# The second layer's normalised rows transposed once, and their sums formed from the transposed quarters

## The chip, the cores and the metric

The kernel runs on one core of one Trainium2 chip. The metric is the time of one execution in microseconds (us) on the device, as the median of several runs; smaller is better. The engines are called by their names in the profile: PE is TensorE's matmul, PEld its weight load, DVE is VectorE, ACT is ScalarE, POOL is GpSimd, SP is SyncE, which here only starts DMAs.

## What is computed

Two layers of an encoder over 512 tokens of width 1024, in float32. Each layer normalises its input, projects it into heads and a gate, runs a token mixer (layer 0: dilated sliding windows; layer 1: grouped-query attention with rotary over a grid), attends to 256 memory tokens, gates the heads and adds an output projection to the residual stream:

```python
for i in range(DEPTH):
    h = rmsnorm(x, norm_g[i])
    mem_h = rmsnorm(mem, mem_norm_g[i])
    proj = einsum('bsd,de->bse', h, w_in[i])           # heads, memory queries, gate
    o_mix = mixer_dilated(...) if i % 2 == 0 else mixer_axial_gqa(...)
    o_mem = memory_attention(q_mem, mem_h, w_mem_kv[i], ...)
    y = concatenate([o_mix, o_mem], axis=-1) * silu(gate)
    x = x + einsum('bse,ed->bsd', y, w_out[i])
```

The change sits between the two layers: where the x that layer 0 has just produced is normalised and brought into the form in which layer 1's projections read it.

## The kernel before

**Split matmuls.** TensorE multiplies in a shortened float32 (fp32r). Every operand is therefore kept as a high part (a rounded copy) and a low part (the value minus the high part), and each product is three matmuls (`mm3`, L162 to L165: high x high, high x low, low x high). `split` (L155) makes the two parts: ScalarE copies the high part, VectorE subtracts it to get the low one.

**Weights.** `Weights` streams weight tiles of 128 x 1024. For each, SP starts the load (`dma`, L233), ScalarE makes the high part `wh` (`hi`, L285), and VectorE the low part `wo` (`lo`, L295). ScalarE can only make the next high part once TensorE is done with the tile four earlier (RING). `advance` (L311) is called after each group of matmuls and issues up to two low parts, one weight sum, up to two high parts and new loads. A group of matmuls with the advance and the tick behind it is called a slot here.

**S chunks.** A large projection is not one matrix product but seven products of quarter matrices (`s_chunk`, L352, in the order of PRODUCTS, L350), as in Strassen's scheme: the activations are cut into four quarters, 11 and 12 (first half of the tokens, first and second half of the columns), 21 and 22 (second half of the tokens), and the seven left operands are 12, 11, S1 = 21 - 22, S2 = S1 - 11, S4 = 12 + S2, S3 = 11 - 21, and 22. The weights have such sums too (T1 to T4); in the later chunks they are formed by DMAs that add onto a tile, started on GpSimd's queue (`sum`, L238: T1 at L247, T2 at L257, T3 at L264, T4 at L269). An activation operand is held with its columns on the partitions, so it has to be transposed, high and low part in one 128 x 2048 tile.

**The order of the work** is written out by the kernel's own driver (`Driver`, L41). Every group of matmuls ends with a `tick`. A generator that was handed over with `spawn` is stepped in a tick, behind the weights' `advance` of that slot; one handed over with `release` has its first step in `free`, which runs right behind the matmuls and in front of `advance`; its later steps run in ticks. What a generator yields is the number of slots until its next step. `late` puts an instruction at the end of the tick, `soon` at the start of the next. Each engine works strictly in the order in which its instructions were written.

**Around the change.** `out_proj` (L810) of layer 0 ends in `out_rest` (L694): `chunk` (L331) runs 2 x 4 groups, one per half n of the columns and block b of 128 tokens, and spawns `ev` per group with a delay of 2, which adds the product to the residual `acc` (L705). For n = 1 it goes on into `ev_o` (L1189): store the block to `x1d` (L1192), sum of squares (ScalarE) and reciprocal root (GpSimd) in `norm_1` (L450), the scaling in `norm_2` (L463, two instructions of VectorE), and then the operands for layer 1. For b < 2 `put_h` (L495) transposes and splits 12 and 11. For b >= 2 `sum_h` (L504) forms S1 in natural layout, `sums_h` (L509) puts S1 and forms S2, S3 and S4 in natural layout, and after the last block `rest_h` (L519) puts S2, S4, S3 and 22, one per slot. Each `put_h` of a block of 128 tokens is four 128 x 128 transposes into a PSUM bank (`turn4`, L467), one ScalarE copy and one VectorE subtraction of 128 x 512. The pauses between the steps are the numbers in EO (L30).

Behind `out_proj` come the memory tokens' projections (`mem_kv`, L593), two times four groups of twelve matmuls: keys (`ev_k`: squares on ScalarE, reciprocal root on GpSimd, scaling on VectorE, transpose, split) and values (`ev_v`: high part, and one slot later the low part, both read from the PSUM bank). `setup_b` (L1221) builds the rotary table of layer 1 in four steps, the first SET_B ticks after its spawn. Then the first S chunk of layer 1 (memory queries, `ev_qmb`) begins with the operand 12.

Of the kernel before, what the change touches and what calls it, by code (L numbers as in the profile page):

```python
# [10 lines left out]
F32 = mybir.dt.float32  # L11
F32R = mybir.dt.float32r
AF = mybir.ActivationFunctionType
ALU = mybir.AluOpType
# [8 lines left out]
NBIG, NM4, NS2, SCRATCH = 7, 23, 13, 2048  # L23
RING, LEAD = 4, 2
XW, BOTH = (1, 2, 0, 5), False
BULK, ACTIVE, MEM_AT, SET_AT, WARM, MEM_B, PREP_Y, ACC_AT, PREP_B, HALF, SET_B = 2, 2, 5, 15, 1, 12, 1, 4, 1, {"a": 3, "b": 3, "o": 0}, 3
MEM_STEP = 1, 1
MEM_D = 4
PD, W_EARLY = 1, True
EO = 1, 2, 2, 2, 1  # L30
YB = {"m": (2, 2), "k": (1, 1, 1), 0: (1, 2, 1), 1: (1, 2, 1)}
Y = [3, 2, 2, 2, 3, 2, 2, 1, 1, 1]

# [91 lines left out]
def trunk_kernel(ctx: ExitStack, tc: tile.TileContext, x, mem, wall, norm_g, mem_norm_g, gcol,  # L125
                 qn_a, kn_a, qn_b, kn_b, ident_d, mask_d, tab_a, tab_b, out):
    nc = tc.nc
    V, A, G, T = nc.vector, nc.scalar, nc.gpsimd, nc.tensor
# [6 lines left out]
    drv = Driver()  # L135

    def big(dt=F32, name="big"):
        return pool.tile([128, 2048], dt, tag="big", name=name, bufs=NBIG)

    def m4(dt=F32, name="m4"):  # L140
        return pool.tile([128, 1024], dt, tag="m4", name=name, bufs=NM4)

    def s2(dt=F32, name="s2"):
        return pool.tile([128, 512], dt, tag="s2", name=name, bufs=NS2)

    def pj(name="pj"):
        return psum.tile([128, 512], F32, tag="pj", name=name, bufs=4)

    def at(name="at"):
        return psum.tile([128, 512], F32, tag="at", name=name, bufs=4)  # L150
# [4 lines left out]
    def split(hi, lo, src, act=True):  # L155
        if act:
            A.copy(hi, src)  # L157
        else:
            V.tensor_copy(hi, src)
        V.tensor_tensor(lo, src, hi.bitcast(F32), ALU.subtract)  # L160
# [170 lines left out]
    def chunk(units, nb, group, evac):  # L331

        ps = [None] * nb
        for u in range(units):
            w = []
            for h, l in (W.take(), W.take()):
                w += [(h[:, k * 512:(k + 1) * 512], l[:, k * 512:(k + 1) * 512]) for k in range(2)]
            for b in range(nb):
                if u == 0:
                    ps[b] = pj()  # L340
                group(w, u, b, ps[b])
                drv.free()
                W.advance()
                if u == units - 1:
                    drv.spawn(evac(b, ps[b]), 2)
                drv.tick()

    n_half = [0]
# [101 lines left out]
    def norm_1(xb, both=False):  # L450

        ss = sm(2, "ss")
        for j in range(2):
            jk = s2(name="sq")
            if both and j:
                V.tensor_tensor_reduce(jk, xb[j], xb[j], 1.0 / 1024.0, 0.0, ALU.mult, ALU.add, ss[:, j:j + 1])
            else:
                A.activation(jk, xb[j], AF.Square, scale=1.0 / 32.0, accum_out=ss[:, j:j + 1])
        r, e = sm(1, "rstd"), sm(1, "mse")
        G.tensor_tensor(e, ss[:, 0:1], ss[:, 1:2], ALU.add)  # L460
        return rstd_of(e, 1)

    def norm_2(xb, r, row, js=(0, 1)):  # L463
        for j in js:
            V.scalar_tensor_tensor(xb[j], xb[j], r, row[j], ALU.mult, ALU.mult)

    def turn4(src, hi, lo, mid=None):  # L467

        p = at("xT")
        for k in range(4):  # L470
            T.transpose(p[:, k * 128:(k + 1) * 128], src[:, k * 128:(k + 1) * 128], ident)  # L471
        if mid:
            mid()
        split(hi, lo, p.rearrange("p (k t) -> p k t", k=4))

    def norm_3(xb, dst, c0, j):
        cs = slice(c0, c0 + 128)
        turn4(xb[j], dst.block(0, j, cs), dst.block(1, j, cs))
# [6 lines left out]
    def proj_t(act, sels, evac):  # L485

        def group(w, u, b, p):
            for k in range(4):
                kk = 4 * u + k
                mm3(p, sels[b](act, 0, kk), sels[b](act, 1, kk), w[k][0], w[k][1], kk == 0, kk == 7)  # L490
        chunk(2, len(sels), group, evac)

    part = {}

    def put_h(H, k, c, src, mid=None, early=False):  # L495

        if c == 0:
            part[k] = big(F32R, "h" + k).rearrange("p (a k t) -> p a k t", a=2, k=4)
        if c or early:
            H[k] = part[k]  # L500
        cs = slice(c * 128, (c + 1) * 128)
        turn4(src, part[k][:, 0, :, cs], part[k][:, 1, :, cs], mid)

    def sum_h(low):  # L504
        s1 = s2(name="xs1")
        V.tensor_tensor(s1, low[0], low[1], ALU.subtract)
        return s1

    def sums_h(H, top, low, c, s1, sums):  # L509

        (a11, a12), a21 = top, low[0]
        s2_, s4 = s2(name="xs2"), s2(name="xs4")
        put_h(H, "S1", c, s1)
        V.tensor_tensor(s2_, s1, a11, ALU.subtract)
        V.tensor_tensor(a21, a11, a21, ALU.subtract)
        V.tensor_tensor(s4, a12, s2_, ALU.add)
        sums.append((s2_, s4, a21, low[1]))

    def rest_h(H, sums, d=1):  # L519
        for i, k in enumerate(("S2", "S4", "S3", "22")):  # L520
            for c in range(2):
                put_h(H, k, c, sums[c][i])
            yield d

    def head_sq(p, n=4):
        ss = sm(n, "hss")
        for j in range(n):
            jk = small.tile([128, 128], F32, tag="junk", name="junk", bufs=2)
            A.activation(jk, p[:, j * 128:(j + 1) * 128], AF.Square, scale=QS, accum_out=ss[:, j:j + 1])  # L529
        return rstd_of(ss, n)  # L530

    def head_mul(p, r, n=4, dst=None):
        xn = (s2(name="xn") if dst is None else dst).rearrange("p (a b) -> p a b", a=4)
        V.tensor_tensor(xn[:, 0:n], p.rearrange("p (a b) -> p a b", a=4)[:, 0:n],  # L534
                        r[:, 0:n, None].to_broadcast([128, n, 128]), ALU.mult)
        return xn

    def transpose4(xn, n=4):
        p = at("qT")
        for j in range(n):  # L540
            T.transpose(p[:, j * 128:(j + 1) * 128], xn[:, j, :], ident)
        return p.rearrange("p (a b) -> p a b", a=4)
# [44 lines left out]
    def put_norm(q, gain, hi, lo):  # L587

        drv.late(lambda: A.activation(hi, q, AF.Copy, scale=gain))
        drv.soon(lambda: V.scalar_tensor_tensor(lo, q, gain, hi.bitcast(F32), ALU.mult, ALU.subtract))  # L590
        yield 1

    def mem_kv(layer, M):  # L593
        kt_ = [m4(F32R, "kmT").rearrange("p (h t) -> p h t", h=4) for _ in range(2)]
        vt_ = [m4(F32R, "vm").rearrange("p (b e) -> p b e", b=2) for _ in range(2)]

        def ev_k(b, p):
            r = head_sq(p)
            yield 2
            xn = head_mul(p, r)  # L600
            yield 2
            q = transpose4(xn)
            cs = slice(b * 128, (b + 1) * 128)
            yield from put_norm(q, gk_m[layer], kt_[0][:, :, cs], kt_[1][:, :, cs])

        def ev_v(b, p):

            A.activation(vt_[0][:, b], p, AF.Copy, scale=0.5)
            yield 1
            V.scalar_tensor_tensor(vt_[1][:, b], p, 0.5, vt_[0][:, b].bitcast(F32), ALU.mult, ALU.subtract)  # L610

        proj_t(M, NAT[:2], ev_k)
        proj_t(M, NAT[:2], ev_v)
        return kt_, vt_
# [238 lines left out]
    H, H2 = {}, {}  # L853
# [3 lines left out]
    def prep():  # L857

        s1, sums = [], []
        for c in range(2):  # L860
            norm_2(xb[2 + c], nst[2 + c], first)
            s1.append(sum_h(xb[2 + c]))
            yield 1
        for c in range(2):
            sums_h(H, xb[c], xb[2 + c], c, s1[c], sums)
            yield 1
        yield from rest_h(H, sums)
# [25 lines left out]
    def mid():  # L893
        busy(128)
        W.lo()
        nst[1] = norm_1(xb[1], BOTH)
# [287 lines left out]
    x1d = dram.tile([4, 128, D], F32, name="x1d", bufs=1)  # L1184
    row_load("x1", norm_g[1:2, :])

    x1b, sums_b = {}, []

    def ev_o(n, b, x1):  # L1189
        if n:  # L1190
            for j in range(2):
                nc.sync.dma_start(x1d[b][:, j * 512:(j + 1) * 512], x1[j])  # L1192
            r = norm_1(x1)
            yield EO[0]
            norm_2(x1, r, rows["x1"])
            x1b[b] = x1
            yield EO[1]
            if b < 2:
                put_h(H2, "12", b, x1[1])
                put_h(H2, "11", b, x1[0])  # L1200
            else:
                s1 = sum_h(x1)
                yield EO[2]
                sums_h(H2, x1b[b - 2], x1, b - 2, s1, sums_b)
            if b == 3:
                yield EO[3]
                yield from rest_h(H2, sums_b, EO[4])

    drv.spawn(mem_norm(1), MEM_B)
    out_proj(YW, ys, xv, ev_o, lambda: [m4(name="acc") for _ in range(2)])  # L1210


# [303 lines left out]
```

## Time and profile before

| what | value |
|---|---|
| median of 3 runs | 973.45 us (973.19 to 974.49) |
| the profiled execution's own time | 971.6 us |
| its span | 969.8 us |
| granted TensorE clock, mean | 1.0 |

The span is the time from the first to the last instruction of the program in the profiled execution. A row of a timeline gives the start in us from the span's start, the duration in us, the engine, the line of the kernel, the operation, what it writes and reads, the shape, how many instructions were merged, and in brackets how long the engine sat idle before it and for what. A row of the waits gives who waited for whom, the total in us, how often, and the longest. A row of the windows gives a stretch, its length, the busy time of PE, PEld, DVE, ACT and POOL (with the number of instructions), the granted clock, the busy share of the DMA engines and GB/s. Starts of successive matmuls tell TensorE's progress better than its busy time, as the ends of matmuls are modelled. A few per cent of the matmul records can be missing.

### The profile page before, as it was taken

To read this page: it belongs to the slowest core of one execution; us is meant where nothing else is said; L and a number is where in the kernel's file an instruction comes from. 1 tells how busy PE (TensorE), PEld (TensorE's weight loads), DVE (VectorE), ACT (ScalarE), POOL (GpSimd) and SP (SyncE) were. 2 spreads that over 40 slices of the span, in tenths; PEclk is the share of its full clock that TensorE was granted. 3 is DMA by queue.
4 is the path that set the end of the run, shared out by engine and by line. 5 is a ranking of instruction groups with operands and counts; after the bars stand their busy time and mean duration, and the time that the engine had idled before them with its cause. 6 is when DMAs were issued, how large, how long until landed. Compare 5 with 4: busy or idle time off the path is not lost. (4 is left out here: it accounts for less than half of the span.)

```text
span 969.8 us, 16665 instructions
## 1 busy us (share of the span) xinstructions
PE 949.5 (98%) x5728; PEld 835.8 (86%) x5728; DVE 793.1 (82%) x1413; ACT 675.4 (70%) x1687; POOL 332.7 (34%) x480
## 2 busy tenths in 40 slices
PE   8899999999999999999999999999999999999998
PEld 5689988888888888888899996787999999998776
DVE  6997776888888888888898999769888997779863
ACT  6555689686868686868685667545778887878760
POOL 1122423556454545454736011323233231011011
PEclk9999999999999999999999999999999999999999
DMA  8979846968787868685959889959986696786644
GB/s 331 326 267 336 220 102 170 293 131 259 150 256 154 256 153 261 154 260 131 279 134 233 259 203 272 299 191 351 240 178 148 178 241 166 218 213 163 183 140 130
DMA packets 88982, 209.27 MB, mean 216 GB/s; under 512 B 25281, under 2 KB 36033, under 8 KB 88898
## 3 DMA queue, kind: packets, MB, share of 16 engines
q1 hardware_dynamic: 70034, 146.28, 43.5%
q0 software_dynamic: 17568, 59.78, 32.5%
q10 hardware_dynamic: 1296, 2.16, 0.6%
q8 instruction: 45, 0.74, 0.3%
q14 instruction: 39, 0.32, 0.1%
HBM read 157.79 MB, written 12.65 MB: 176 GB/s over the span
## 5 line engine op out<-in xcount | busy, mean ns | idle before, releaser
L295 DVE TENSOR_TENSOR wo<-wl,wh 128x1024 fp32r<-128x1024 f32 x255 | 314.6, 1237 | 12.3 <-ACT wh L285 11.5
L285 ACT CAST wh<-wl 128x1024 fp32r<-128x1024 f32 x255 | 269.7, 1059 | 75.7 <-PE pj L165 39.8
L163 PE MATMUL pj<-wh,hS 128*128 128x512 f32 (+1 forms) x448 | 164.3, 367 | 0.0
L164 PE MATMUL pj<-wo,hS 128*128 128x512 f32 (+1 forms) x448 | 158.1, 353 | 2.6 <-DVE wo L295 2.6
L165 PE MATMUL pj<-wh,hS 128*128 128x512 f32 (+1 forms) x448 | 158.2, 353 | 0.0
L163 PE MATMUL pj<-wh,h 128*128 128x512 f32 (+1 forms) x336 | 123.4, 367 | 0.0
L164 PE MATMUL pj<-wo,h 128*128 128x512 f32 (+1 forms) x336 | 118.8, 354 | 2.3 <-DVE wo L295 2.3
L165 PE MATMUL pj<-wh,h 128*128 128x512 f32 (+1 forms) x336 | 118.9, 354 | 0.0
L420 POOL TENSOR_TENSOR rstd<-mse,half 128x4 f32<-128x4 f32 (+2 forms) x98 | 100.1, 1021 | 8.2
L164 PEld LDWEIGHTS pj<-wo,hS 128*128 128x128 f32 x448 | 85.0, 190 | 13.4 <-DVE wo L295 3.5
L165 PEld LDWEIGHTS pj<-wh,hS 128*128 128x128 f32 x448 | 84.7, 189 | 12.4 <-DVE hS L160 0.3
L163 PEld LDWEIGHTS pj<-wh,hS 128*128 128x128 f32 x448 | 84.8, 189 | 9.7
L419 POOL TENSOR_SCALAR mse<-hss 128x4 f32<-128x4 f32 (+1 forms) x86 | 44.3, 515 | 129.9 <-ACT junk L529 126.1
L360 ACT COPY sn<-pj 128x512 f32<-128x512 f32 x132 | 73.6, 591 | 14.3 <-PE pj L165 10.7
L529 ACT ACTIVATE junk<-sn 128x128 f32<-128x128 f32 x264 | 79.0, 308 | 0.2 <-DVE sn L371 0.2
L987 POOL TENSOR_TENSOR ta<-sn,tabs 128x128 f32<-128x128 f32 (+1 forms) x64 | 37.2, 584 | 119.7 <-DVE sn L534 91.6
L164 PEld LDWEIGHTS pj<-wo,h 128*128 128x128 f32 x336 | 64.0, 190 | 10.0 <-DVE wo L295 2.8
L165 PEld LDWEIGHTS pj<-wh,h 128*128 128x128 f32 x336 | 63.7, 190 | 9.3 <-DVE h L160 0.2
L163 PEld LDWEIGHTS pj<-wh,h 128*128 128x128 f32 x336 | 63.9, 190 | 7.3 <-ACT h L157 0.2
L377 DVE TENSOR_TENSOR sn<-pj,sn 128x512 f32<-128x512 f32 x99 | 67.5, 683 | 3.0 <-PE pj L165 2.6
L269 POOL DMA_DIRECT2D wl<-wl x33 | 29.3, 886 | 112.4 <-DVE wo L295 70.7
L163 PE MATMUL pj<-hS,wh 128*128 128x256 f32 x192 | 55.9, 291 | 0.0
(229 smaller groups left out, 2457.1 us busy)
## 6 DMA issues: line engine op xcount, KB each, us to landing
wl<-in_wall_dram SPq DMA_DIRECT2D x222, 512.0 KB, 6.9
wl<-wl POOLq DMA_DIRECT2D x64, 512.0 KB, 5.8
wl<-in_wall_dram POOLq DMA_DIRECT2D x42, 512.0 KB, 8.5
acc<-sn POOLq DMA_DIRECT2D x16, 256.0 KB, 5.0
od<-o SPq DMA_DIRECT2D x12, 256.0 KB, 5.2
og<-od SPq DMA_DIRECT2D x12, 256.0 KB, 6.8
odb<-o SPq DMA_DIRECT2D x12, 256.0 KB, 2.7
og<-odb SPq DMA_DIRECT2D x12, 256.0 KB, 3.9
```

The source lines that it names most:

```text
L163: T.matmul(o, lh, rh, start=start, stop=False, skip_group_check=True)
L164: T.matmul(o, lh, rl, start=False, stop=False, skip_group_check=True)
L165: T.matmul(o, ll, rh, start=False, stop=stop, skip_group_check=True)
L269: G.dma_start(self.tile[key], self.tile[c, "T2", x], accum_op=ALU.add)
L285: A.copy(wh, self.tile[self.items[i]])
L295: V.tensor_tensor(wo, self.tile[key], wh.bitcast(F32), ALU.subtract)
L360: A.copy(t, b)
L377: V.tensor_tensor(t, b, t, ALU.subtract if q == "12" else ALU.add)
L419: G.tensor_scalar(e, ss, EPS, None, ALU.add)
L420: G.tensor_tensor(r, e, half[:, 0:n], ALU.pow)
L529: A.activation(jk, p[:, j * 128:(j + 1) * 128], AF.Square, scale=QS, accum_out=ss[:, j:j + 1])
L987: G.tensor_tensor(ta[:, 0:n], xn[:, 0:n, 0:32], ropeA[:, 0, b, s0:s0 + n], ALU.mult)
```

## The change

Layer 0's output still comes block by block through `ev_o`. Now each normalised half block is transposed once. `first_t` (b < 2) transposes and splits 12 and 11 and also copies the unsplit transposed quarter from the bank into SBUF (`whole`, tiles of 128 x 1024 in the weights' pool). `diffs_t` (b >= 2) copies the transposed 22 to SBUF, takes the transposed 21 from its bank, forms S1 = 21 - 22 and S3 = 11 - 21 in transposed form, and splits S1. `rest_t` forms S2 and S4 over both blocks at once (128 x 1024) and splits S2, S4, S3 and 22 at that width, one per slot. `put_h`, `sum_h`, `sums_h` and `rest_h` stay for the first layer.

`chunk` hands its evacuations over with `release`, in front of `W.advance()`, instead of `spawn` behind it: in both layers' memory projections and both `out_rest`. In `ev_v` the low part goes to the end of the tick of the same slot (`late`) instead of the next slot. EO and SET_B change: normalising comes one slot later, the step after it follows after two slots, S2 to 22 come one slot earlier than before, and the rotary table starts two slots earlier.

```diff
--- before.py
+++ after.py
@@ -23,11 +23,11 @@
 NBIG, NM4, NS2, SCRATCH = 7, 23, 13, 2048
 RING, LEAD = 4, 2
 XW, BOTH = (1, 2, 0, 5), False
-BULK, ACTIVE, MEM_AT, SET_AT, WARM, MEM_B, PREP_Y, ACC_AT, PREP_B, HALF, SET_B = 2, 2, 5, 15, 1, 12, 1, 4, 1, {"a": 3, "b": 3, "o": 0}, 3
+BULK, ACTIVE, MEM_AT, SET_AT, WARM, MEM_B, PREP_Y, ACC_AT, PREP_B, HALF, SET_B = 2, 2, 5, 15, 1, 12, 1, 4, 1, {"a": 3, "b": 3, "o": 0}, 1
 MEM_STEP = 1, 1
 MEM_D = 4
 PD, W_EARLY = 1, True
-EO = 1, 2, 2, 2, 1
+EO = 2, 2, 1, 1, 1
 YB = {"m": (2, 2), "k": (1, 1, 1), 0: (1, 2, 1), 1: (1, 2, 1)}
 Y = [3, 2, 2, 2, 3, 2, 2, 1, 1, 1]
 
@@ -340,9 +340,9 @@
                     ps[b] = pj()
                 group(w, u, b, ps[b])
                 drv.free()
+                if u == units - 1:
+                    drv.release(evac(b, ps[b]), 2)
                 W.advance()
-                if u == units - 1:
-                    drv.spawn(evac(b, ps[b]), 2)
                 drv.tick()
 
     n_half = [0]
@@ -469,9 +469,12 @@
         p = at("xT")
         for k in range(4):
             T.transpose(p[:, k * 128:(k + 1) * 128], src[:, k * 128:(k + 1) * 128], ident)
+        p = p.rearrange("p (k t) -> p k t", k=4)
         if mid:
             mid()
-        split(hi, lo, p.rearrange("p (k t) -> p k t", k=4))
+        if hi is not None:
+            split(hi, lo, p)
+        return p
 
     def norm_3(xb, dst, c0, j):
         cs = slice(c0, c0 + 128)
@@ -521,6 +524,56 @@
             for c in range(2):
                 put_h(H, k, c, sums[c][i])
             yield d
+
+
+    full = {}
+
+    def whole(k, c):
+        if c == 0:
+            full[k] = m4(name="f" + k).rearrange("p (k t) -> p k t", k=4)
+        return full[k][:, :, c * 128:(c + 1) * 128]
+
+    def slot(H, k, c):
+        if c == 0:
+            part[k] = big(F32R, "h" + k).rearrange("p (a k t) -> p a k t", a=2, k=4)
+        else:
+            H[k] = part[k]
+        cs = slice(c * 128, (c + 1) * 128)
+        return part[k][:, 0, :, cs], part[k][:, 1, :, cs]
+
+    def first_t(H, top, c):
+
+        ps = [(k, turn4(top[j], *slot(H, k, c))) for k, j in (("12", 1), ("11", 0))]
+        for k, p in ps:
+            A.copy(whole(k, c), p)
+
+    def diffs_t(H, low, c):
+
+        f22 = whole("22", c)
+        A.copy(f22, turn4(low[1], None, None))
+        p = turn4(low[0], None, None)
+        yield 1
+        s1, s3 = whole("S1", c), whole("S3", c)
+        V.tensor_tensor(s1, p, f22, ALU.subtract)
+        V.tensor_tensor(s3, full["11"][:, :, c * 128:(c + 1) * 128], p, ALU.subtract)
+        split(*slot(H, "S1", c), s1)
+
+    def rest_t(H, d):
+        def put(k, f):
+            H[k] = big(F32R, "h" + k).rearrange("p (a k t) -> p a k t", a=2, k=4)
+            split(H[k][:, 0], H[k][:, 1], f)
+
+        s2_, s4 = full["11"], full["12"]
+        V.tensor_tensor(s2_, full["S1"], s2_, ALU.subtract)
+        put("S2", s2_)
+        yield d
+        V.tensor_tensor(s4, s4, s2_, ALU.add)
+        put("S4", s4)
+        yield d
+        put("S3", full["S3"])
+        yield d
+        put("22", full["22"])
+        yield d
 
     def head_sq(p, n=4):
         ss = sm(n, "hss")
@@ -606,8 +659,8 @@
         def ev_v(b, p):
 
             A.activation(vt_[0][:, b], p, AF.Copy, scale=0.5)
-            yield 1
-            V.scalar_tensor_tensor(vt_[1][:, b], p, 0.5, vt_[0][:, b].bitcast(F32), ALU.mult, ALU.subtract)
+            drv.late(lambda: V.scalar_tensor_tensor(vt_[1][:, b], p, 0.5, vt_[0][:, b].bitcast(F32), ALU.mult, ALU.subtract))
+            yield 1
 
         proj_t(M, NAT[:2], ev_k)
         proj_t(M, NAT[:2], ev_v)
@@ -1184,7 +1237,6 @@
     x1d = dram.tile([4, 128, D], F32, name="x1d", bufs=1)
     row_load("x1", norm_g[1:2, :])
 
-    x1b, sums_b = {}, []
 
     def ev_o(n, b, x1):
         if n:
@@ -1193,18 +1245,14 @@
             r = norm_1(x1)
             yield EO[0]
             norm_2(x1, r, rows["x1"])
-            x1b[b] = x1
             yield EO[1]
             if b < 2:
-                put_h(H2, "12", b, x1[1])
-                put_h(H2, "11", b, x1[0])
+                first_t(H2, x1, b)
             else:
-                s1 = sum_h(x1)
+                yield from diffs_t(H2, x1, b - 2)
+            if b == 3:
                 yield EO[2]
-                sums_h(H2, x1b[b - 2], x1, b - 2, s1, sums_b)
-            if b == 3:
-                yield EO[3]
-                yield from rest_h(H2, sums_b, EO[4])
+                yield from rest_t(H2, EO[3])
 
     drv.spawn(mem_norm(1), MEM_B)
     out_proj(YW, ys, xv, ev_o, lambda: [m4(name="acc") for _ in range(2)])
```

## The prediction

> **What bounds the kernel now.** I read the page's busy line first, then TensorE's waits, then the stretches around the change, then the timelines of the queues there.
>
> ```profile
> PE 949.5 (98%) x5728; PEld 835.8 (86%) x5728; DVE 793.1 (82%) x1413; ACT 675.4 (70%) x1687; POOL 332.7 (34%) x480
> ```
> ```profile
> PE ob L164 <- DVE pbT L1357: 2.4, 2, 1.3
> PE pj L165 <- DVE y L752: 1.3, 1, 1.3
> ```
> ```profile
> 647.60:660.30 12.70, 12.70 (x65) 10.69 (x65) 8.40 (x11) 9.96 (x20) 4.80 (x10) 1.00 0.99 379
> 660.30:672.90 12.60, 12.09 (x57) 9.61 (x55) 12.56 (x19) 7.35 (x22) 5.79 (x6) 1.00 1.04 353
> 672.90:694.00 21.10, 20.43 (x170) 19.83 (x170) 19.78 (x28) 14.21 (x29) 3.48 (x4) 1.00 0.94 279
> ```
>
> TensorE is the bound: busy for 98% of the span. The two wait rows are all its waits from 690 us to the end, 3.7 us, so what the change wins or loses by 690 us lasts. The three stretches hold the second layer's memory projection and its first S chunk. From 660.3 to 672.9 VectorE (third busy number) works 12.56 of 12.60 us: there it, not TensorE, decides how late things are. The DMA engines are full (0.99, 1.04, 0.94).
>
> TensorE and VectorE in that place:
>
> ```profile
> 653.11 1.03 PE L471 MATMUL xT<-ident,acc 128*128 128x128 f32 x8
> 653.90 0.48 PE L163 MATMUL pj<-wh,act 128*128 128x512 f32 x1
> 654.21 0.40 PE L164 MATMUL pj<-wo,act 128*128 128x512 f32 x1
> 654.44 0.39 PE L165 MATMUL pj<-wh,act 128*128 128x512 f32 x1
> ...
> 656.72 1.03 PE L471 MATMUL xT<-ident,acc 128*128 128x128 f32 x8
> ...
> 665.77 0.60 PE L471 MATMUL xT<-ident,xs 128*128 128x128 f32 x4
> 666.13 0.48 PE L163 MATMUL pj<-wh,act 128*128 128x512 f32 x1
> 667.12 0.50 PE L164 MATMUL pj<-wo,act 128*128 128x512 f32 x1 [0.51 <-DVE wo L295]
> ...
> 674.19 0.38 PE L164 MATMUL pj<-wo,h 128*128 128x256 f32 x1 [0.29 <-DVE wo L295]
> ...
> 678.42 0.63 PE L541 MATMUL qT<-ident,xn 128*128 128x128 f32 x4 [0.35 <-DVE xn L534]
> ...
> 682.56 0.36 PE L163 MATMUL pj<-wh,hS 128*128 128x256 f32 x1
> ...
> 685.51 1.03 PE L471 MATMUL xT<-ident,acc 128*128 128x128 f32 x8
> ...
> 690.04 0.36 PE L163 MATMUL pj<-wh,hS 128*128 128x256 f32 x1
> ```
> ```profile
> 651.45 1.41 DVE L465 SCALAR_TENSOR_TENSOR acc<-acc,rstd,row 128x512 f32<-128x512 f32 x2 [1.23 <-ACT sq L458]
> 652.78 0.68 DVE L705 TENSOR_TENSOR acc<-pj,acc 128x512 f32<-128x512 f32 x1
> 654.92 1.29 DVE L160 TENSOR_TENSOR h<-xT,h 128x512 fp32r<-128x512 f32 x2 [1.45 <-ACT h L157]
> 657.65 1.42 DVE L465 SCALAR_TENSOR_TENSOR acc<-acc,rstd,row 128x512 f32<-128x512 f32 x2 [1.45 <-DMA x1d<-acc]
> ...
> 665.85 2.35 DVE L295 TENSOR_TENSOR wo<-wl,wh 128x1024 fp32r<-128x1024 f32 x2
> 668.12 0.68 DVE L506 TENSOR_TENSOR xs<-acc 128x512 f32<-128x512 f32 x1
> 668.72 0.68 DVE L1225 TENSOR_TENSOR tabs<-tbraw,grB 128x512 f32<-128x512 f32 x1
> ...
> 685.98 1.20 DVE L295 TENSOR_TENSOR wo<-wl,wh 128x1024 fp32r<-128x1024 f32 x1
> ```
>
> I call a slot the matmuls between two weight advances, and the eight slots of the memory projection p0 to p7; the seven of the S chunk are q0 to q6 (products 12, 11, S1, S2, S4, S3, 22). Eight transposes push the next matmul out by 653.90 - 653.11 = 0.79 us, and the step behind them is 0.31 instead of 0.23: 0.87 us in all. Four cost 0.36 + 0.08 = 0.44. A p slot takes 656.72 - 653.90 - 0.09 = 2.73 us, a q slot 685.51 - 682.56 - 0.08 = 2.87. So p0 starts at 653.11 - 2 x 2.73 = 647.65. Up to q4 (690.04) these make 8 x 2.73 + 4 x 2.87 of products, 6 x 0.87 of double transposes and 4 x 0.44 of single ones (two for S1, two for the keys): 40.3 us. It takes 42.4. The missing **2.1 us** are TensorE waiting for VectorE, at the three bracketed rows above all (a bracket counts only from the modelled end of the matmul before; the starts lie further apart).
>
> **The change, part by part.**
>
> ```profile
> L471 PE MATMUL xT<-ident,acc x32: 270/272/273, 653.1 to 690.0; 128*128 128x128 f32 x32
> ```
>
> *Transposes.* Before there are 14 turns of four transposes: four for 12 and 11, two for S1, eight for S2, S4, S3, 22. After there are eight: two per token block. Gone are 2 x 0.44 + 4 x 0.87, added 2 x 0.87: **-2.6 us** on TensorE, on the path. [...]
>
> *VectorE and ScalarE steps.* Prices, start to start without a wait: a 512-column tensor_tensor 0.60 (668.12 to 668.72), one of 1024 columns 1.13 (two from 665.85 to 668.12), a normalising step 0.67 (two in 1.41 with a tail). A 1024-wide sum or split from SBUF does not run in the trace in this role; its bounds are the wo row (1.13) and two 512s (1.20); I take 1.13, the same form. VectorE's columns are equal: before 14 lows and 8 sums of 512, after 10 of 512 and 6 of 1024, 13.2 against 12.8 us. ScalarE gets more: 12 copies of 512 and 4 of 1024 instead of 14 of 512. What changes is the order.
>
> *First half (p0 to p7): better.* The rope table (four 0.60 and a 0.25) starts two slots earlier, and the last block's residual add is emitted in front of p0's weight split instead of at 652.78. Both go into VectorE's idle 1.23, 1.45 and 1.45 us. The two plain s1 differences and six plain sums leave p3 to p6 (p5 and p6 get the S1 and S3 differences instead). So the wo of p6 comes before it is needed and the three waits go: **-2.1 us**. I laid the queues out one after the other at these prices, each instruction behind its predecessor and its inputs; the same layout for the kernel before puts q4 at 690.02 (measured 690.04). After, it gives q0 at 673.2, q1 at 676.5, q2 at 679.5, on the clock of before.
>
> *Second half (q0 to q4): worse.*
>
> ```profile
> 671.78 1.05 ACT L285 CAST wh<-wl 128x1024 fp32r<-128x1024 f32 x1 [0.81 <-PE pj L165]
> 676.85 1.05 ACT L285 CAST wh<-wl 128x1024 fp32r<-128x1024 f32 x1 [4.02 <-DMA wl<-wl]
> ```
> ```profile
> 657.90 0.95 POOL L247 DMA_DIRECT2D wl<-in_wall_dram  x1
> ...
> 667.33 0.93 POOL L257 DMA_DIRECT2D wl<-wl  x1 [2.42 <-DMA wl<-in_wall_dram]
> 668.33 0.56 POOL L419 TENSOR_SCALAR mse<-hss 128x4 f32<-128x4 f32 x1
> 668.98 1.34 POOL L420 TENSOR_TENSOR rstd<-mse,half 128x4 f32<-128x4 f32 x1
> ```
>
> At p7 ScalarE has to make the high part of weight T2, which waits for an accumulating DMA; it landed at 676.8, 9.5 us after its issue at 667.33, which itself waited for the one of 657.90. The change puts S2's high part right behind this on ScalarE, and VectorE, which reaches the S2 difference at 674.6 and is through it at 675.7, queues S2's low part in front of the value's low part and of the wo of T1 and T2. T1's accumulation is emitted behind the last block's norm, whose squares no longer stand behind two copies on ScalarE: about 1 us earlier. T2's, however, now stands on Pool behind the second key block's rstd (moved to the front of its slot; its squares end on ScalarE at 664.3, Pool's two steps above take 2.1), and starts at 666.4. So T2 lands at 675.8, its cast and S2's own (0.95 apart) put S2's low part at 677.9 (VectorE idle 2.2), the value's low part runs to 679.6, wo of T1 is complete at 680.8, and q2, reached at 679.5, loses **1.2 us**.
>
> Then VectorE owes wo of T2, the first key's low part (0.67, the normalising form), the S4 sum (1.13), a round trip through ScalarE (a cast of 1.05, 1.2 idle), S4's low part, the second value's and key's low parts, S3's low part (0.55 idle, 1.13; before it stood behind weight 22) and the add of product 11, all in front of the wo of weight 22. That starts at 689.6 (before 685.98) and is complete at 690.8. q4, reached at 686.6, gets its second matmul then: **4.1 us** lost. Behind it the S chunk's VectorE work per q slot (a wo and an add, 1.73) is under 2.87, so nothing more is lost.
>
> *At nothing.* The same reordering of first steps touches the first layer's memory projection and both output projections. TensorE does not wait between the first two of these rows, nor from the third to 667.12:
>
> ```profile
> 38.99 0.50 PE L164 MATMUL pj<-wo,hS 128*128 128x512 f32 x1 [0.16 <-DVE wo L295]
> 156.00 0.66 PE L666 MATMUL pmt<-ident,pm 128*128 128x128 f32 x4 [0.59 <-ACT pm L649]
> ...
> 629.22 1.33 PE L471 MATMUL xT<-ident,m 128*128 128x128 f32 x8 [0.28 <-issue]
> ```
>
> The cover there is weights split ahead; if it were gone, each slot would lose up to an eviction, 0.60. On SP the last block's stores to x1d no longer wait for the add of 652.78, so the weight loads behind them go out earlier by up to 3 us; five more quarter tiles (12, 11, 22, S1, S3) come from the pool of the weights, while the four x tiles return sooner, so I take no loss on the loads. The value's low part frees its bank for q2 at 679.7, inside q2's 1.2.
>
> **The sum.** -2.6 - 2.1 + 1.2 + 4.1 = **+0.6 us**. The profiled execution took 971.6 (span 969.8, 1.8 around it); the runs' median is 973.45, 0.2% above it. The offset carries over: 973.45 + 0.6 = **974.0**.
>
> **Rivals.** (1) *VectorE's gaps close.* If S2's and S4's high parts come without holding VectorE up (T2 landing before 674.9, and casts that end while VectorE still has other work), the idle 2.2 + 1.2 + 0.55 us go: 974.0 - 3.9 = 970.1. For it: equal VectorE columns, and idle time in front to absorb work. With no wait at all it would be 973.45 - 4.7 = 968.8. Against: from 647.9 to the wo of 22 VectorE owes 20 steps of 0.60, 10 of 0.67, 16 of 1.13 and 0.25, 37.0 us, which end at 684.9 at the earliest, and q4 would want them at 685.3.
> (2) *The accumulated weight comes later (slower).* From a landing at about 674.9 on, each us that T2 is late moves S2's low part, the wo of T1 and q2 by one us. The place is Pool's T2 issue behind the key rstd, which waits for ScalarE, now fuller by the quarter copies. 3 us later: 974.0 + 3 = 977.0. For it: DMA at 0.94 to 1.04, and the DMA's 9.4 us. Against: ScalarE is only 7.35 of 12.60 busy.
> (3) *The clock falls.*
>
> ```profile
> 2.24 3.75 PE L562 MATMUL row<-row,ones 1*128 1x512 f32 x4 [2.24 <-DMA row<-in_norm_g_dram]
> ...
> 10.25 0.63 PE L164 MATMUL pj<-wo,h 128*128 128x512 f32 x1
> 10.68 0.63 PE L165 MATMUL pj<-wh,h 128*128 128x512 f32 x1
> ```
>
> The wait of 4.1 us at q4 would be longer than the one of 2.24 at the start, the longest in the trace. At the start matmuls of 512 stand 0.43 apart (10.25, 10.68) instead of 0.23. Six to thirteen such behind the wait cost 1.2 to 2.6, say 1.7: 975.7. [...] The granted clock here is 1.00 in every stretch; no wait that long is in this trace.
>
> **How the numbers follow.** A measurement of this kernel tells about 0.2% (1.9 us) from no change. My forecast gets 0.45 and lies inside that (own range 972.5 to 975.4); rival 1 0.28 (faster), rival 2 0.22, rival 3 0.05 (both slower). Range 970.0 to 977.0: from rival 1 without its ideal end to rival 2 with 3 us. Faster 0.28, same 0.45, slower 0.27.
>
> **What would show it.** The profile after should have 32 transposes with x1 as source where before had 56; no wait of TensorE between 660 and 673; the S2 sum on VectorE followed by an idle stretch that ends with ScalarE; a wait at q2 and a longer one at q4, both for the wo of L295; T2's cast waiting for a DMA until about 676. If q4 starts before 686 and waits under 2 us, rival 1 holds; if q2's wait exceeds 3 us, rival 2; if matmuls behind q4's wait stand 0.4 apart, rival 3. The forecast is wrong if VectorE's low parts are emitted in another order than I read from the driver's slots.

## The result, and the profile after

The changed kernel takes **980.06 us** (median of 6 runs, 978.27 to 982.37) against 973.79 us for the kernel before in the same session (6 runs, 971.29 to 974.72): a ratio of 1.0068, 95% interval 1.0054 to 1.0082. It is slower by 6.3 us, where 974.0 was forecast and 977.0 was the upper end of the range. The profiled execution took 978.27 us (span 976.4), 6.7 more than the one before.

First the page's busy line. The columns are as before the change.

```profile
PE 952.1 (98%) x5704; PEld 838.7 (86%) x5704; DVE 793.2 (81%) x1407; ACT 678.3 (69%) x1689; POOL 337.9 (35%) x480
```

TensorE has 5704 matmuls instead of 5728: the 24 transposes are gone. Still its busy time is higher by 2.6 us, although it has less to do. That points to slower matmuls. Next the first row of TensorE's waits (who waited for whom, us in total, times, longest), and the timeline of TensorE around the change:

```profile
PE pj L163 <- ACT h L157: 6.6, 2, 5.9
```
```profile
679.33 0.35 PE L163 MATMUL pj<-wh,hS 128*128 128x256 f32 x1
680.36 0.39 PE L164 MATMUL pj<-wo,hS 128*128 128x256 f32 x1 [0.69 <-DVE wo L295]
...
683.10 0.28 PE L165 MATMUL pj<-wh,hS 128*128 128x256 f32 x1
689.27 0.55 PE L163 MATMUL pj<-wh,hS 128*128 128x256 f32 x1 [5.89 <-ACT h L157]
689.62 0.41 PE L164 MATMUL pj<-wo,hS 128*128 128x256 f32 x1
689.84 0.41 PE L165 MATMUL pj<-wh,hS 128*128 128x256 f32 x1
...
695.17 0.32 PE L163 MATMUL pj<-wh,hS 128*128 128x256 f32 x1
695.33 0.28 PE L164 MATMUL pj<-wo,hS 128*128 128x256 f32 x1
695.45 0.28 PE L165 MATMUL pj<-wh,hS 128*128 128x256 f32 x1
```

Up to q2 the forecast holds: q2 starts at 679.33 (forecast 679.5), and its second matmul, due 0.20 later, comes at 680.36, 0.8 us late for a wo (forecast 1.2). Then there is a row that the forecast did not have: **q3** stands still from 683.10 to 689.27. Behind it the matmuls of 256 columns start 0.21 apart (689.62, 689.84) instead of 0.12 (695.33, 695.45), until 695.17. The view by windows shows the same as a granted clock of 0.79 (the last three numbers are clock, DMA share and GB/s):

```profile
684.00:700.00 16.00, 10.73 (x67) 10.76 (x68) 10.86 (x12) 10.35 (x20) 4.45 (x4) 0.79 0.98 292
```

q3 starts at 689.27. What ended just before it? VectorE's and ScalarE's timelines:

```profile
682.02 1.22 DVE L570 TENSOR_TENSOR f<-f,f 128x1024 f32<-128x1024 f32 x1
684.35 1.23 DVE L160 TENSOR_TENSOR hS<-f,hS 128x1024 fp32r<-128x1024 f32 x1 [1.11 <-ACT hS L157]
...
687.30 1.23 DVE L160 TENSOR_TENSOR hS<-fS,hS 128x1024 fp32r<-128x1024 f32 x1 [0.47 <-ACT hS L157]
688.44 0.68 DVE L377 TENSOR_TENSOR sn<-pj,sn 128x512 f32<-128x512 f32 x1
689.04 1.22 DVE L295 TENSOR_TENSOR wo<-wl,wh 128x1024 fp32r<-128x1024 f32 x1
```
```profile
683.27 1.04 ACT L157 CAST hS<-f 128x1024 fp32r<-128x1024 f32 x1 [4.88 <-DVE f L570]
...
684.80 0.57 ACT L360 COPY sn<-pj 128x512 f32<-128x512 f32 x1
...
688.11 1.05 ACT L157 CAST h<-f 128x1024 fp32r<-128x1024 f32 x1
```

Two things end within 0.04 us of each other. ScalarE's cast of 22 (688.11) ends at 689.16, and the profile names it. VectorE's `sn<-pj,sn` (688.44), the add that evacuates product 11, ends at 689.12. The wo of weight 22 for which the forecast had q4 wait starts at 689.04, close to the forecast (689.6). So VectorE's queue was laid out rightly, and the wait came one product earlier, for another instruction of the same queue.

**The theory.** In PRODUCTS the entry of S2 is not fresh: product S2 adds onto the PSUM bank that holds product 11. Before q3's first matmul may write there, VectorE's add must have read it. That add is written at the end of q2, but VectorE reaches it only behind S4's sum and low part, two more low parts, and S3's low part; it also needs ScalarE's copy of product 12 (684.80), which stands behind S4's cast. Before the change the same add ran at 685.38 to 686.05, and q3 started at 686.30: no wait, but no slack either. Its rows, and q3's, in the kernel before:

```profile
685.38 0.67 DVE L377 TENSOR_TENSOR sn<-pj,sn 128x512 f32<-128x512 f32 x1
686.30 0.36 PE L163 MATMUL pj<-wh,hS 128*128 128x256 f32 x1
```

The idle 6 us then take the clock down (0.79 in the window above). **Rival A**: the row is right, and q3 waits for ScalarE's cast of 22. **Rival B**: VectorE has too much to do here in any order. **Rival C**: the release part of the change does it, not the transposed sums.

### The profile page after: what moved, and what is told of

It is laid out like the page before. It is cut to its first block, busy times and chain, and to the rows that moved or that the text cites. A ratio compares the mean times of both kernels' runs of the same rounds, so it can differ in the third digit from the quotient of the medians.

```text
span 976.4 us, 16618 instructions
## 1 busy us (share of the span) xinstructions
PE 952.1 (98%) x5704; PEld 838.7 (86%) x5704; DVE 793.2 (81%) x1407; ACT 678.3 (69%) x1689; POOL 337.9 (35%) x480
## 4 chain that ended last, share of the span: by engine, by line
PE 82%; DMA 7%; DVE 7%; ACT 3%; issue 1%; SPq 1%; DVEq 0%; ACTq 0%
PE pj L165 21%; PE pj L164 21%; PE pj L163 21%; PE qT L594 2%; DMA og<-od 2%; DVE wo L295 2%; PE oo L1198 1%; PE sa L1096 1%; PE ptb L1396 1%; PE pt L1177 1%; PE sa L1092 1%; DMA wl<-in_wall_dram 1%; DMA og<-odb 1%; PE xT L471 1%; DMA oth<-ds 1%
## 5 line engine op out<-in xcount | busy, mean ns | idle before, releaser
L295 DVE TENSOR_TENSOR wo<-wl,wh 128x1024 fp32r<-128x1024 f32 x255 | 314.2, 1236 | 10.9 <-ACT wh L285 10.4
L163 PEld LDWEIGHTS pj<-wh,hS 128*128 128x128 f32 x448 | 86.2, 192 | 15.8 <-ACT h L157 6.1
L165 PEld LDWEIGHTS pj<-wh,hS 128*128 128x128 f32 x448 | 86.0, 192 | 12.3 <-DVE hS L160 0.2
```

The costliest lines, as they stand in the source:

```text
L163: T.matmul(o, lh, rh, start=start, stop=False, skip_group_check=True)
L165: T.matmul(o, ll, rh, start=False, stop=stop, skip_group_check=True)
L295: V.tensor_tensor(wo, self.tile[key], wh.bitcast(F32), ALU.subtract)
```

## The experiments

All times are compared with those of the kernel before, taken beside them on the same chip (its median was 971.80, 973.03 and 972.59 us in the three sessions). Since p0 starts at 646.2 to 648.6 us in these profiles, places in a profile are counted from p0, its first matmul with the memory tokens: "q3 at" is q3's first matmul, "queries at" the first transposes of the memory queries (in the profile a PE row `qT<-ident,sn`), 54 us behind p0, where all of this is over.

| kernel | ratio to before (95%) | q3 at | queries at | last matmul at |
|---|---|---|---|---|
| before | 1 | 38.64 | 53.97 | 317.82 |
| after | 1.0068 (1.0054 to 1.0082) | 41.89 | 58.98 | 324.74 |
| late22 | 1.0081 (1.0050 to 1.0111) | 41.91 | 58.17 | 325.77 |
| fill | 1.0045 (1.0021 to 1.0069) | 41.91 | 56.38 | 323.88 |
| order | 1.0008 (0.9992 to 1.0024) | 36.64 | 52.79 | 318.99 |
| ownbank | 1.0035 (1.0019 to 1.0052) | 39.52 | 55.90 | 322.90 |
| turns | 1.0071 (1.0059 to 1.0083) | 45.62 | 60.18 | 326.65 |
| release | 0.9983 (0.9973 to 0.9992) | 37.95 | 53.28 | 317.25 |
| soon | 0.9994 (0.9984 to 1.0005) | 37.12 | 53.00 | 318.59 |
| soon_acc | 0.9957 (0.9944 to 0.9970) | 36.56 | 51.69 | 315.57 |
| before_acc | 0.9981 (0.9969 to 0.9993) | 38.93 | 54.26 | 316.87 |
| soon_fill | 0.9948 (0.9931 to 0.9966) | 36.55 | 51.69 | 314.03 |

### Is it the add or the cast? (late22)

```diff
         put("S3", full["S3"])
-        yield d
+        yield 3
         put("22", full["22"])
```

> The changed kernel with 22's split two slots later (behind the wo of T3), nothing else moved. Theory: the fourth product (q3, operand S2) adds onto the PSUM bank of product 11, so it waits for VectorE's add that reads this bank; that add stands ahead of 22's split, so q3 still starts about 42 us after p0 (689.3 in the profile after), with 5.5 to 6 us of wait, and the time stays within 1 us of the changed kernel's (978 to 981). Rival A: the profile's row is right, and q3 waits for ScalarE's cast of 22 (ended 689.16). That cast now stands behind q3's part of the order, so the wait at q3 goes: q3 about 35.5 to 36.5 us after p0, and 974 us.

Measured: ratio 1.0081, 979.84 us; q3 at 41.91, where after has it at 41.89. TensorE's row, VectorE's add and ScalarE's cast of 22 in this profile:

```profile
688.16 0.55 PE L163 MATMUL pj<-wh,hS 128*128 128x256 f32 x1 [5.89 <-DVE sn L377]
```
```profile
687.33 0.68 DVE L377 TENSOR_TENSOR sn<-pj,sn 128x512 f32<-128x512 f32 x1
```
```profile
694.53 1.05 ACT L157 CAST h<-f 128x1024 fp32r<-128x1024 f32 x1
```

The cast of 22 now starts at 694.53, 6 us behind q3's start, and q3 hasn't moved. With the cast out of the way the same wait of 5.89 us is put down to the add, which ends at 688.01. Rival A is refuted: the row of after named the instruction that happened to end last.

### What does the clock cost? (fill)

```diff
+    def fill():
+        p = at("fill")
+        for n in range(44):
+            T.matmul(p[:, 0:256], H2["S1"][:, 0, 0, 0:128], H2["S1"][:, 0, 0], start=n == 0, stop=n == 43, skip_group_check=True)
...
                 bank[s] = [pj() for _ in range(units)]
+            if fill and i == 3:
+                fill()
```

> The changed kernel with 44 extra matmuls of 256 columns into a spare bank in front of q3 (5.2 us of TensorE work, results unused). Theory: q3 still starts about 42 us after p0, since VectorE's add sets it, but the clock no longer falls: matmuls behind q3's start stand 0.12 apart instead of 0.21, and the time is 2 to 3 us under the changed kernel's (about 977.5). Rival: the wide spacing has nothing to do with idle time (contention with the weight transfers or with VectorE): the spacing stays at 0.21 and the time at 980.

Measured: ratio 1.0045, 977.19 us; TensorE, and the window that showed 0.79 in after:

```profile
682.65 5.44 PE L1317 MATMUL fill<-hS 128*128 128x256 f32 x44
688.72 0.36 PE L163 MATMUL pj<-wh,hS 128*128 128x256 f32 x1 [0.63 <-ACT h L157]
688.91 0.28 PE L164 MATMUL pj<-wo,hS 128*128 128x256 f32 x1
689.03 0.28 PE L165 MATMUL pj<-wh,hS 128*128 128x256 f32 x1
```
```profile
684.00:700.00 16.00, 15.37 (x129) 15.20 (x128) 13.02 (x14) 12.16 (x28) 4.44 (x4) 1.00 0.98 290
```

q3 is at 41.91, as in after (41.89), with 5.2 us of useless work where TensorE had stood still, and the matmuls behind it stand 0.12 apart. The queries come at 56.38 instead of 58.98: the fall of the clock costs **2.6 us** in after's profile. By medians of one session the gain over late22, which has the same wait, is 979.84 - 977.19 = 2.65; the intervals of the two ratios overlap, so it is the profile that shows the size.

### Is it the order or the amount? (order)

```diff
         put("S2", s2_)
-        yield d
+        yield 3
         V.tensor_tensor(s4, s4, s2_, ALU.add)
         put("S4", s4)
```

> The changed kernel with S4, S3 and 22 two slots later, behind the add of product 11, and one slot apart as before. Theory: the add then follows the first key's and the second value's low parts, q3 waits 0 to 1.5 us and starts about 37 us after p0, the later products wait under 1 us each, matmuls stay 0.12 apart, and the time is 0.2 to 1.5 us under the kernel before (ratio 0.9985 to 1.000), since the transposes and the waits of the first half are still gained. Rival B: VectorE simply has too much to do here, and the wait goes to q4, q5 or q6 instead, 4 us or more in sum: 977 to 979 us.

Measured: ratio 1.0008 (972.54 us), q3 at 36.64, clock 1.00. VectorE and TensorE:

```profile
683.41 0.68 DVE L377 TENSOR_TENSOR sn<-pj,sn 128x512 f32<-128x512 f32 x1
684.01 1.22 DVE L295 TENSOR_TENSOR wo<-wl,wh 128x1024 fp32r<-128x1024 f32 x1
685.14 1.22 DVE L570 TENSOR_TENSOR f<-f,f 128x1024 f32<-128x1024 f32 x1
```
```profile
684.15 0.38 PE L163 MATMUL pj<-wh,hS 128*128 128x256 f32 x1 [0.63 <-DVE sn L377]
687.98 0.39 PE L163 MATMUL pj<-wh,hS 128*128 128x256 f32 x1 [0.69 <-ACT sn L360]
688.76 0.39 PE L165 MATMUL pj<-wh,hS 128*128 128x256 f32 x1 [0.28 <-DVE hS L160]
```

The same instructions, with S4's three behind the add, and the 6 us are gone; the three waits that remain from q3 on add up to 1.6. Rival B is refuted. At the queries the kernel is 1.2 us ahead of before, as expected. But the time is not: the ratio lies just above the expected one (0.9985 to 1.000), which its interval overlaps. In the profile, by the last matmul, the 1.2 us have turned into a loss of 1.2. Where it goes is below (soon).

### Taking the bank away (ownbank)

```diff
         for i, (a, s, fresh) in enumerate(PRODUCTS):
...
+            fresh = fresh or own and i == 3
             if fresh:
                 bank[s] = [pj() for _ in range(units)]
```

> The changed kernel with a PSUM bank of its own for product S2 instead of product 11's, so that q3 has no bank to wait for; the sums over products that need S2 on top of 11 are left out. VectorE's order is untouched. Theory: q3 starts about 36 us after p0, and the wait goes to q4, as the prediction had it: q4 waits 3.5 to 5 us for the wo of weight 22, complete at about 42.8 us after p0. Without the clock's fall this is 975 us, with it 977.5. Rival A, that q3 waits for a ScalarE cast: q3 doesn't move and the time stays at 980.

Measured: ratio 1.0035, 975.76 us, inside the expected times; but the place is not the expected one.

```profile
680.41 0.36 PE L163 MATMUL pj<-wh,hS 128*128 128x256 f32 x1 [1.30 <-DVE vm L663]
681.45 0.39 PE L164 MATMUL pj<-wo,hS 128*128 128x256 f32 x1 [0.68 <-DVE wo L295]
686.52 0.55 PE L163 MATMUL pj<-wh,hS 128*128 128x256 f32 x1 [2.06 <-ACT sn L360]
```
```profile
676.41 1.05 ACT L285 CAST wh<-wl 128x1024 fp32r<-128x1024 f32 x1 [1.57 <-DMA wl<-wl]
```
```profile
689.53 0.68 DVE L377 TENSOR_TENSOR sn<-pj,sn 128x512 f32<-128x512 f32 x1
```

q3 now starts at 686.52, 3 us **ahead** of the add (689.53) and ahead of the cast of 22 too. So without the shared bank it waits for neither. It was expected 3.5 us earlier still. About 1.5 us of that was lost ahead of it: in this execution weight T2 landed later (ScalarE waits 1.57 us for it, where it did not wait in after), S2's low part and the value's low part came later, and q2 started at 33.41 behind p0 instead of 31.95. The rest is another bank: the bank that it gets instead is the one of product 12, and ScalarE's copy out of that bank stands behind S4's cast, which itself waits for VectorE's S4 sum (the row at 683.27 in after shows this chain). q4 then comes so late that it hardly has to wait for the wo of weight 22. That the wait would go to q4 is not shown.

### One part at a time (turns, release)

turns keeps the transposed sums alone (the edit below taken back, SET_B 3, and EO 1, 2, 2, 1, 1, so that S2 stays in its slot). release is the kernel before with the other part alone, SET_B 1 and this edit:

```diff
                 drv.free()
+                if u == units - 1:
+                    drv.release(evac(b, ps[b]), 2)
                 W.advance()
-                if u == units - 1:
-                    drv.spawn(evac(b, ps[b]), 2)
...
             A.activation(vt_[0][:, b], p, AF.Copy, scale=0.5)
+            drv.late(lambda: V.scalar_tensor_tensor(vt_[1][:, b], p, 0.5, vt_[0][:, b].bitcast(F32), ALU.mult, ALU.subtract))
             yield 1
-            V.scalar_tensor_tensor(vt_[1][:, b], p, 0.5, vt_[0][:, b].bitcast(F32), ALU.mult, ALU.subtract)
```

> The kernel after with chunk's spawn, the value's low part one slot later and SET_B 3 as before; only the transposed sums remain. Theory: the add of product 11 still stands behind the 1024-wide low parts of S4 and S3, so q3 waits 4 to 6.5 us, the clock falls behind it, and the ratio is 1.005 to 1.009. Rival C: without the release part the wait at q3 is under 2 us and the ratio 0.998 to 1.002.

> The kernel before with only the release of chunk's evacuations, the value's low part at the end of the same tick and the rotary table two slots earlier (SET_B 1); the turns of four transposes and the sums stay in the old layout. By the prediction's terms: the waits at p6, q0 and q1 go, 2.1 us at most, and nothing is lost at q3, since S4 and S3 stay 512 wide and S3 behind the add's slot: ratio 0.9978 to 0.9995. Rival C: this part is what costs (the value's low part in front of the weights pushes the wo of q2 or the add of product 11 later): ratio 1.002 to 1.006, with waits at q2 or q3.

Measured: turns 1.0071, as slow as the whole change; release 0.9983, 1.7 us faster. Rival C is refuted: the transposed sums cost, the release part gains. In release only the row `[0.41 <-DVE wo L295]` at p6 is left of the three waits of before. But turns isn't slow in the place that was expected (TensorE, then ScalarE):

```profile
674.83 0.63 PE L594 MATMUL qT<-ident,xn 128*128 128x128 f32 x4 [1.48 <-DVE xn L587]
...
687.76 0.58 PE L163 MATMUL pj<-wh,hS 128*128 128x256 f32 x1 [4.07 <-ACT sn L360]
```
```profile
685.12 1.04 ACT L157 CAST hS<-f 128x1024 fp32r<-128x1024 f32 x1 [4.28 <-DVE f L570]
...
687.13 0.58 ACT L360 COPY sn<-pj 128x512 f32<-128x512 f32 x1
```

Part of its loss comes early: without the release part, TensorE waits 1.48 us for the first key, the matmuls of 256 columns behind it stand 0.21 apart up to 679.71, and q1 starts 33.16 behind p0, where before has it at 31.15 and after at 29.00. Then it is **q2** that stands still, for the copy of product 12 on ScalarE, whose bank product S1 gets in this order of releases; q3 comes at 45.62, when the add is done. So the theory has to be put more widely. The evacuations of the first two products, a copy on ScalarE and an add on VectorE, stand in their queues behind S4's chain (sum on VectorE, cast on ScalarE, low part on VectorE). Which product stops for it depends on who gets which bank.

### Can the sums be placed without the wait? (soon, soon_acc, before_acc, soon_fill)

```diff
     def put(k, f):
         H[k] = big(F32R, "h" + k).rearrange("p (a k t) -> p a k t", a=2, k=4)
-        split(H[k][:, 0], H[k][:, 1], f)
+        hi, lo = H[k][:, 0], H[k][:, 1]
+        A.copy(hi, f)
+        drv.soon(lambda: V.tensor_tensor(lo, f, hi.bitcast(F32), ALU.subtract))
...
     put("S2", s2_)
-    yield d
+    yield 2
```

> The changed kernel with the low parts of S2, S4, S3 and 22 at the start of the tick behind their cast (behind the next weight's low part on VectorE instead of in front of it), and S4, S3 and 22 one slot later, S4's sum directly ahead of the add of product 11. Theory: VectorE no longer stands still for ScalarE's casts; q2 doesn't wait for the wo of T1, q3 waits 1 to 1.5 us for the add, the clock stays, and the last product (q6) starts 44.5 to 45.5 us after p0, where the kernel before needs 48.2. If all of that reaches the end: 3 to 3.6 us under the kernel before (ratio 0.9963 to 0.997). Rival D: what is won here is lost again behind 905 us, where VectorE waits for the loads of the attention's output (2.55 us in the kernel before, 3.97 in the order run): ratio 0.999 to 1.001.

soon_acc also starts the x1d loads of the last output projection three ticks later:

```diff
-        drv.spawn(load(), ACC_AT)
+        drv.spawn(load(), at_)
...
-    out_proj(YW, ys, x1d, ev_o2, acc_b, HALF.get("o"))
+    out_proj(YW, ys, x1d, ev_o2, acc_b, HALF.get("o"), ACC_AT + 3)
```

> As soon, and the last output projection's loads of x1d start three ticks later, so that the second load of the attention's output stands ahead of them on SP. Rival D: that load lands 1.5 to 4 us earlier, the wait of TensorE for VectorE's add near 913 us goes, and the gain of soon reaches the end: ratio 0.996 to 0.998, and at least 1 us under soon. If the gain of soon reaches the end anyway: same as soon, or slower if the x1d loads now come too late for the first sums.

Measured: soon 0.9994, soon_acc **0.9957**, 2.7 us under soon by medians. Rival D was right. In soon the queries are 1.0 us ahead of before, and less was won than expected (q6 at 47.2, expected 44.5 to 45.5): q3 still waits 2.13 us for the add, and in this execution the clock falls behind it (matmuls of 256 columns 0.21 apart) until 687.05. soon_acc, with the same code up to there, waits 1.57 us, keeps its clock (0.12 apart), and has q6 at 45.9. Then the tail. VectorE in soon, and in soon_acc:

```profile
905.39 0.68 DVE L802 TENSOR_TENSOR sn<-sn,og 128x512 f32<-128x512 f32 x1
910.20 0.69 DVE L802 TENSOR_TENSOR sn<-sn,og 128x512 f32<-128x512 f32 x1 [4.13 <-DMA og<-odb]
```
```profile
905.51 1.45 DVE L802 TENSOR_TENSOR sn<-sn,og 128x512 f32<-128x512 f32 x2
```

In soon, as in before (2.55 us) and order (3.97), VectorE stops for the second load of the attention's output. SP issues it between 904.17 and 904.38 in all three, although order and soon are a us ahead at the queries, behind a first load of x1d; what holds SP there is not shown. TensorE's waits for VectorE's add at 912.80 (soon, 1.66 us) and at 913.46 (order, 1.50 us) follow it. With the x1d loads moved behind it the waits are gone.

before_acc is the kernel before with this last edit alone; soon_fill is soon_acc with the extra matmuls of fill, ten instead of 44:

```diff
-        for n in range(44):
+        for n in range(10):
```

> The kernel before with only the last output projection's x1d loads three ticks later. Rival D (the tail waits for the second load of the attention's output): in the kernel before VectorE waits 2.55 us for that load, but no wait of TensorE behind 905 us names the add, so this alone is worth little: ratio 0.9985 to 1.0005, and soon_acc's 0.9957 is mostly the sums'. If instead the loads alone are the gain, the ratio is 0.996 to 0.998.

> soon_acc with 10 extra matmuls of 256 columns (1.2 us, results unused) in front of q3, where TensorE waits 1.6 to 2.1 us for the add of product 11. If the clock falls in some executions behind such a wait (1.23 us lost in the profile of soon, none in that of soon_acc), the extra matmuls keep it up and the time is 0 to 1 us under soon_acc: ratio 0.995 to 0.9965. If the wait is too short to matter, the extra matmuls cost what they overrun: 0 to 0.5 us over soon_acc.

before_acc alone gives 0.9981, more than "little" and so only partly as expected: 1.8 us. The expectation looked for a wait of TensorE that names the add; the one that it missed names VectorE's next product. In before, VectorE's `pbT` of 915.95, late behind that load, keeps TensorE waiting 1.15 us at 916.68; in before_acc it starts at 913.30, and this wait is gone. soon_acc's 0.9957 is then about half the loads' and half that of the rest of the change (0.9957 / 0.9981 = 0.9976). The rest holds the release part, which alone gave 0.9983. So no run shows that the transposed sums, even in this order, gain anything of their own: release with the later loads was not run. soon_fill gives **0.9948** (967.13 us), the fastest kernel here, 5.1 us under before; its interval (0.9931 to 0.9966) overlaps that of soon_acc, so the gain of the ten extra matmuls is not established.

## Why the prediction was wrong

By its own steps, in the profile of after:

- *Transposes, -2.6 us*: right in number (5704 instead of 5728). Their time isn't measured alone.
- *First half, -2.1 us*: right. TensorE doesn't wait from the start of p0 to q2, and q0, q1 and q2 start within 0.2 us of the forecast. release alone gained 1.7 us (0.8 to 2.6) in time, but its profile is only 0.7 us ahead at q3 (37.95 instead of 38.64), so not all of the 2.1 us is had without the transposed sums.
- *q2, +1.2 us*: right in place and cause, 0.8 in size. Weight T2 landed a little earlier than the forecast 675.8: ScalarE made its high part without a wait for it, in the two casts from 674.17 to 676.31. That was luck in part: in ownbank, with the same order up to there, it did wait for T2 (1.57 us), and q2's second matmul came 2.3 us late.
- *q4, +4.1 us for the wo of weight 22*: **this is the step that failed.** "the add of product 11" is in the prediction's list of what VectorE owes ahead of that wo, and it was costed only as 0.60 us of VectorE. That q3 accumulates onto the bank which this add reads was left out, so q3's condition was missing from the layout. With this one link put in, the prediction's own numbers give the wait: q3 is reached at 683.6 (679.5 + 1.2 + 2.87), and the add ends about where the wo of weight 22 starts, at 689.6, so q3 loses 6.0 us (measured: 689.27 less 683.10 and one step of 0.12, 6.05).
- *Rival 3, the clock*: its mechanism came, at q3 instead of q4. It was priced at 1.7 us with a chance of 0.05, and it costs 2.6. Its six to thirteen slowed matmuls were the author's estimate; behind q3's wait of 5.89 us in after, 26 steps from matmul to matmul take 0.21 instead of 0.12 (689.62 to 695.17). The prediction itself had its wait of 4.1 us longer than the 2.24 us of the start, with matmuls of 512 columns 0.43 apart instead of 0.23 behind that one; so the clock should have been part of the sum, not a rival.
- *Rival 1* did not happen in after: VectorE stood still 1.11, 1.11 and 0.47 us for ScalarE's casts. The order soon removes these, and its queries are 1.0 us ahead of before. *Rival 2* did not happen in after.

The sum by the measured terms: -2.6 - 2.1 + 0.8 + 6.1 + 2.6 = +4.8, against 58.98 - 53.97 = +5.0 at the queries. The profiled execution is 6.7 longer in all. The rest lies at the end: a wait of 0.53 us at 948.85 and a second fall of the clock (1.6 us) behind 950 us. That fall also shows in the profiles of late22, fill, ownbank and soon_acc, and not in those of turns, order, soon and soon_fill; whether any of these kernels has it in every execution is not shown by one profile each. None of the three kernels without the transposed sums (before, release, before_acc) shows it there, so whether the change makes it more frequent is not shown; the kernel before loses clock in some executions too (granted clocks of 0.996 to 1.000 in its 21 runs beside late22). How much of the medians' 6.3 us it makes up stays open.

## What to carry to other kernels

When work is moved in an engine's queue, look at each instruction behind it for what it frees, not only for what it costs: an evacuation of 0.6 us that was just in time, with TensorE writing the same bank 0.25 us later, turned into 6 us. Put long chains that go back and forth between two engines (sum, cast, low part) behind the evacuations that the next product needs, and emit the last link one slot later, so that VectorE has other work while ScalarE casts. Add the slower clock to every forecast wait of several us: behind those of 4.07 us (turns) and 5.89 us (after, late22) matmuls of 256 columns stood 0.21 apart instead of 0.12, which cost 2.6 us in after. And when a gain in the middle doesn't reach the end, look for a load whose issue did not move with it (904.17 in soon, 904.30 in before).

## What the runs showed of the hardware

**The profile's releaser was the one that ended last.** In after, a cast that ended at 689.16 got the whole 5.89 us, and the cause, ended 0.04 us earlier, got none. Moving the suspect told them apart.

**The clock fell behind short waits too, but not each time.** The same wait of 1.30 or 1.31 us on the last projection, TensorE's rows in before and in after:

```profile
945.62 0.50 PE L165 MATMUL pj<-wh,y 128*128 128x512 f32 x1 [1.31 <-DVE y L752]
945.96 0.40 PE L163 MATMUL pj<-wh,y 128*128 128x512 f32 x1
946.20 0.39 PE L164 MATMUL pj<-wo,y 128*128 128x512 f32 x1
```
```profile
950.65 0.50 PE L165 MATMUL pj<-wh,y 128*128 128x512 f32 x1 [1.30 <-DVE y L805]
...
951.22 0.59 PE L164 MATMUL pj<-wo,y 128*128 128x512 f32 x1
951.62 0.63 PE L165 MATMUL pj<-wh,y 128*128 128x512 f32 x1
...
954.60 0.43 PE L163 MATMUL pj<-wh,y 128*128 128x512 f32 x1
```

In before the matmuls go on 0.23 apart; in after they stand 0.40 to 0.43 apart from 951.22 to 954.60, which costs 1.6 us. This place shows the fall in 5 of the 12 profiles (after, late22, fill, ownbank, soon_acc), after waits of the same length, and the wait of 2.13 us in soon brought it while that of 1.57 in soon_acc did not. Nor does the length alone decide: a wait of 1.48 us brought it in turns (at 674.83), and one of 1.48 us in late22 (at 917.28) did not. The slow stretches behind q2 or q3 last 3.2 to 4.0 us in soon, ownbank and late22, and 5.7 (behind q2's wait) and 5.9 in turns and after. The one behind 951.22 in after lasts 3.38 us. What sets the start and the length of such a stretch is not shown.
